# Mamba-2 decay on ScalarE, and one step between VectorE's results and ScalarE's use of them

## The chip, the cores and the metric

The kernel runs on one core of a Trainium2 chip. A core has several engines, each with its own instruction queue that is worked off in order: TensorE (PE, matrix products; PEld are its weight loads), VectorE (DVE), ScalarE (ACT), GpSimd (POOL), and SyncE (SP), which here issues the loads of weights. Instructions of different engines wait for one another through semaphores. The metric is the device time of one execution in microseconds; the time of a kernel is the median over its runs.

## What is computed

The reference is a two-layer trunk over 256 tokens of width 2048: a Mamba-2 layer with a gated feed-forward block, then a block-sparse attention layer with another such block. The change concerns the Mamba-2 mixer alone, and in it the part that works on 64 heads in chunks of 128 tokens:

```
zxbcdt = x @ w_in                       # z, then x, b, c, then dt
xbc = silu(causal_dwconv(xbc, conv_w, conv_b))
dt = softplus(dt + dt_bias); a = -exp(a_log)
...
a_cum = cumsum(a * dt, axis=2)          # per chunk of 128 tokens
seg = a_cum[:, :, :, None] - a_cum[:, :, None, :]
decay_in = exp(where(causal, seg, -inf))
cb = einsum('bclgn,bcsgn->bclsg', c, b)
y_diag = einsum('bclsgr,bcsgrp->bclgrp', cb[..., None] * decay_in, x)
...
y = (y_diag + y_off) + d_skip * xs
y = y * silu(z)
yg = yg * rsqrt(mean(square(yg)) + eps) # over the 512 channels of a head group
y = (yg * norm_w) @ w_out
```

The 64 heads form 8 head groups of 8 heads (512 channels). Since a_cum falls along a chunk, seg is not positive where the mask lets it through.

## The kernel before

**Steps.** The whole kernel is one list of steps. A step takes one tile of weights, 128 x 1024 numbers (512 KB), loaded by SyncE into the buffer `raw` (L170). Because the products are done in a reduced float format, each tile is cut in two: ScalarE copies it to its high part `hi` (L184), VectorE subtracts this from the tile and leaves the low part `lo` (L185). The activations are cut in the same way. In the steps of the Mamba input projection (the function `whole`) TensorE multiplies the high part with both parts of the activations (L244, 8 products of 128x512) and the low part with the high activations (L246, 8 products of 128x256). Steps of even number within a chunk do L244 first, steps of odd number L246 first. Around three eighths of step i, `splits` issues the cutting of a later tile; 4 buffers of each part let the cutting run at most three steps ahead of the product. In the output projection and later (`half`) the three kinds of product stand on L207, L208 and L212.

**Order.** Nothing is scheduled by a planner: the author writes the order by hand. `at(i, f, ...)` appends a function to the list that is run behind the products of step i, and the functions of one step are issued in the order in which they were appended. Each engine then works through its own instructions in that order. So a piece that is put "at step i" stands, on VectorE and ScalarE, behind the cutting issued in step i and ahead of that issued in step i + 1; whoever waits there holds up all later cutting.

**A head group.** Group g has 16 steps from s0 on: 8 for its x columns (chunk `chX[g]`), 8 for its z columns (`chZ[g]`). A chunk's columns come in two halves, ready after 4 and after 8 steps. Some of a group's work reaches into the 16 steps of the next group, or, for the last group, into the output projection `chO`. The pieces that the change touches or that the prediction needs:

- `m_load` (s0+3): GpSimd issues two transfers that spread a_cum of the 8 heads over all partitions into two tiles `mA` of 128 x 8 x 128, one for each chunk of tokens, c = 0 and 1 (L670). They wait until the diagonal products of the group before have read these buffers.
- `m_cb` (s0+6): the products of b and c (L676, L677); VectorE masks them with a triangle into `cb` (L679); ScalarE copies the third into `bc` (L683).
- `m_into` (s0+6): exponentials of a_cum itself for the state that enters chunk 1 (L696), read from `mA` before it is changed; a load of the activation table stands ahead of them.
- `m_decay` (s0+6 for c = 0, s0+7 for c = 1): a subtraction with a broadcast column for each head (L688) and a minimum with 0 (L689), both on VectorE over the whole tile; then `m_exp` one step later each (L700), and `m_mask` (L704), which multiplies the tile by `cb`, at s0+13 and s0+14.
- the convolution over x: `gather` takes a half of the columns out of the accumulators (L554 on ScalarE, L555 on VectorE), a step later `taps` does the first tap on ScalarE (L577) and three on VectorE (L582). `x_silu` follows at s0+11 (L711, with a table load ahead).
- `x_turn` (s0+13): 8 transposes (L720), then xdt and xe on VectorE (L722, L723); `y_d`, 4 pieces on ScalarE (L729).
- `z_silu`: the gather of a half of z and its silu (L757), at s0+12 and s0+16.
- `y_off`, `y_diag` (s0+18): products L746, L737 and the sums L749, L750, L740 on VectorE.
- `z_gate` (s0+20): y times silu(z) on VectorE (L761), its square on ScalarE (L762); `z_sum` (s0+21) adds the squares (L766, L767); `z_rms` (s0+22) takes their mean over the partitions by a product (L773) and GpSimd does the power; `z_diag` (s0+23, L782).
- `z_scale` for group g is put at step s0+13 of group g + 1 (s0+26 for the last group): one product (L787), four pieces on VectorE (L790), then the high and low parts of the result, the copy on ScalarE (L793) and the subtraction on VectorE (L794), which waits for the copy.

Of the kernel before, what the change touches and what calls it, by code (L numbers as in the profile page):

```python
# [20 lines left out]
AF = mybir.ActivationFunctionType  # L21
OP = mybir.AluOpType
AX = mybir.AxisListType

P = 128
# [5 lines left out]
NG = 8  # L31
# [60 lines left out]
def yoco_kernel(ctx: ExitStack, tc: tile.TileContext, x, lmg, lmb, lfg, lfb, x_t, columns, w, out):  # L92
    nc = tc.nc
# [7 lines left out]
    def t4k(name):  # L101
        return t4.tile([P, 2, NC], F32, tag="t4k", name=name)
# [4 lines left out]
    def tp_tile():  # L107
        return psum.tile([P, NC], F32, tag="tp", name="tp", bufs=2)
# [11 lines left out]
    def c1(name, j):  # L120
        i = COL_AT[name] + j
        return cols[:, i:i + 1]
# [174 lines left out]
    def at(i, f, *a):  # L297
        post.setdefault(i, []).append((f, a))
# [172 lines left out]
    chX, chZ = [], []  # L471
# [76 lines left out]
    aux = mp.tile([P, 5, NH], F32, name="aux")  # L548

    def gather(ch, half, dst, scale=None):  # L550

        p = ch.part[half]
        if scale is None:
            nc.scalar.copy(dst, p[:, :, S:])  # L554
            nc.vector.tensor_add(dst, dst, p[:, :, :S])  # L555
        else:
            nc.scalar.activation(dst, p[:, :, S:], AF.Copy, scale=scale)
            nc.vector.scalar_tensor_tensor(dst, p[:, :, :S], scale, dst, op0=OP.mult, op1=OP.add)
# [36 lines left out]
    def conv4(ch, j, dst, jd):  # L595

        return Conv(ch, j, dst, jd, [k * 48 for k in range(4)], "cw", "cb")
# [58 lines left out]
    G = [dict() for _ in range(NG)]  # L656
# [27 lines left out]
        G[g]["cb"], G[g]["bc"] = cb, bc  # L684

    def m_decay(g, c):
        t = G[g]["A", c]
        nc.vector.tensor_sub(t, t, aux[:, 2 + c, 8 * g:8 * g + 8].unsqueeze(2).to_broadcast([P, 8, P]))  # L688
        nc.vector.tensor_scalar(t, t, 0.0, None, op0=OP.min)  # L689

    def m_into(g):

# [4 lines left out]

    def m_exp(g, c):
        t = G[g]["A", c]
        nc.scalar.activation(t, t, AF.Exp)  # L700

    def m_mask(g, c):
        t = G[g]["A", c]
# [2 lines left out]
    def x_new(g):  # L706
        G[g]["xc"] = mp.tile([P, 4, S], F32, tag="xc", name="xc")
        return G[g]["xc"]
# [40 lines left out]
        nc.vector.tensor_mul(e, e, ps.rearrange("p (j l) -> p j l", l=P))  # L749
        nc.vector.tensor_add(y, y, e)  # L750

    def z_silu(g, half):
        if half == 0:
            G[g]["sz"] = t4k("sz").rearrange("p a (k t) -> p (a k) t", t=S)
        sz = G[g]["sz"][:, 2 * half:2 * half + 2, :]
        gather(chZ[g], half, sz)
        nc.scalar.activation(sz, sz, AF.Silu)  # L757

    def z_gate(g):
        y, sz = G[g]["y"], G[g]["sz"]  # L760
        nc.vector.tensor_mul(y, y, sz)  # L761
        nc.scalar.activation(sz, y, AF.Square)  # L762

    def z_sum(g):
        sz = G[g]["sz"]
# [18 lines left out]
    def z_scale(g):  # L784

        ps = tp_tile()
        nc.tensor.matmul(ps[:, :S], ones, G[g]["rd"].rearrange("p h t -> p (h t)"), start=True, stop=True)  # L787
        y = G[g]["y"]
        for i in range(4):
            nc.vector.scalar_tensor_tensor(y[:, i, :], y[:, i, :], c1("nw", 4 * g + i), ps[:, :S], op0=OP.mult,  # L790
                                           op1=OP.mult)
        hi, lo = (yT[:, 4 * g:4 * g + 4, a, :] for a in range(2))
        nc.scalar.copy(hi, y)  # L793
        nc.vector.tensor_sub(lo, y, hi.bitcast(F32))  # L794
# [8 lines left out]
    for g in range(NG):  # L803
        s0 = chX[g].first
        at(s0 + 3, m_load, g)
        at(s0 + 6, m_cb, g)
        at(s0 + 6, m_into, g)
        at(s0 + 6, m_decay, g, 0)
        at(s0 + 7, m_decay, g, 1)
        at(s0 + 7, m_exp, g, 0)  # L810
        at(s0 + 8, m_exp, g, 1)
        conv4(chX[g], 4 * g, lambda g=g: x_new(g), 0).plan()
        at(s0 + 11, x_silu, g)
        at(s0 + 13, m_mask, g, 0)
        at(s0 + 14, m_mask, g, 1)
        if g:
            at(s0 + 13, z_scale, g - 1)
        at(s0 + 13, x_turn, g)
        at(s0 + 13, y_d, g)
        for b in range(2):  # L820
            at(chZ[g].ready(b), z_silu, g, b)
        at(s0 + 18, y_off, g)
        at(s0 + 18, y_diag, g)
        at(s0 + 20, z_gate, g)
        at(s0 + 21, z_sum, g)
        at(s0 + 22, z_rms, g)
        at(s0 + 23, z_diag, g)
    at(s0 + 26, z_scale, NG - 1)


    def chain(norm, nxt=None, after=None):
# [299 lines left out]
```

## Time and profile before

| | us |
|---|---|
| median of 3 runs | 2583.18 |
| lowest, highest | 2579.88, 2583.73 |
| the profiled execution, its run time | 2580.0 |
| the profiled execution, span from its first to its last instruction | 2578.1 |

The profile is of one execution. The Mamba input projection's head groups take the stretch from about 90 to 525 us of it, with work of the last group until about 566 us. Over 54 us of one group in the middle (226 to 280 us) TensorE is busy 51.17 us, VectorE 42.38, ScalarE 31.34 and GpSimd 2.52; the 16 DMA engines are busy 0.55 of the time. In the next projections of the same form (745 to 1200 us) TensorE is busy all of the 455 us. Times in the views are microseconds from the start of the span, unless they are marked or known as nanoseconds (minimum, median and maximum of one instruction are in nanoseconds). In the view that lists instructions in order of time each row has the start, the length, the engine, the line and operation, what it writes and reads with shapes, and how many like instructions were merged; a bracket gives the idle time of that engine just before, and what ended it. A product's end is modelled and overlaps the next one, so busy times of TensorE are somewhat long and its idle times somewhat short.

### The profile page before, as it was taken

How to read it: one execution, taken by the hardware profiler on the slowest of the kernel's cores; microseconds unless marked ns; L12 is line 12 of the kernel's file. 1: busy time of each engine (PE TensorE's matmuls, PEld its weight loads, DVE VectorE, ACT ScalarE, POOL GpSimd, SP SyncE). 2: the span in 40 equal slices, each digit the busy share in tenths (PEclk: the TensorE clock that was granted, in tenths of full speed). 3: DMA queues.
4: the chain of work that ended last, by engine and by line, in shares of the span. 5: the costliest groups of instructions: out<-in, count | busy, mean ns of one | idle time of the engine just before them, and what ended most of it. 6: DMA issues, size and time to landing. Idle time of an engine off the chain costs nothing.

```text
span 2578.1 us, 36030 instructions
## 1 busy us (share of the span) xinstructions
PE 2545.9 (99%) x14031; PEld 2207.3 (86%) x14031; DVE 1680.7 (65%) x2154; ACT 1313.4 (51%) x1633; POOL 71.6 (3%) x89
## 2 busy tenths in 40 slices
PE   9999999999999999999999999999999999999998
PEld 8888888888888888888888888888888888888887
DVE  7877777774576676666444745655777676665555
ACT  6665555543355555555333444544455555554333
POOL 0000000000010000000000200000200000000001
PEclk9999999999999999999999999999999999999999
DMA  7555555557666556565676665456665555566665
GB/s 261 190 183 168 187 181 164 171 188 228 213 206 194 187 189 189 187 193 184 204 227 198 224 191 180 153 166 217 233 196 188 188 188 190 187 195 198 203 221 163
DMA packets 141498, 501.01 MB, mean 194 GB/s; under 512 B 15616, under 2 KB 16128, under 8 KB 141328
## 3 DMA queue, kind: packets, MB, share of 16 engines
q1 hardware_dynamic: 136976, 483.45, 58.2%
q0 software_dynamic: 4064, 14.75, 1.8%
q8 instruction: 110, 1.80, 0.3%
q14 instruction: 60, 0.49, 0.1%
q10 hardware_dynamic: 288, 0.52, 0.1%
HBM read 490.20 MB, written 8.45 MB: 193 GB/s over the span
## 4 chain that ended last, share of the span: by engine, by line
PE 88%; DVE 6%; ACT 3%; issue 2%; DMA 0%; DVEq 0%; SPq 0%; ACTq 0%
PE acc L244 35%; PE acc L246 18%; PE acc L208 11%; PE acc L212 11%; PE acc L207 11%; DVE lo L185 2%; ACT hi L184 2%; PE acc L737 1%; DVE xc L582 1%; DVE y L790 0%; PE tp L212 0%; PE tp L208 0%; PE tp L207 0%; DVE y L761 0%; DVE yT L794 0%
## 5 line engine op out<-in xcount | busy, mean ns | idle before, releaser
L185 DVE TENSOR_TENSOR lo<-raw,hi 128x1024 fp32r<-128x1024 f32 (+1 forms) x871 | 1063.8, 1226 | 763.2 <-ACT hi L184 759.3
L184 ACT CAST hi<-raw 128x1024 fp32r<-128x1024 f32 (+1 forms) x871 | 908.8, 1048 | 863.8 <-PE acc L212 365.8
L244 PE MATMUL acc<-hT,hi 128*128 128x512 f32 x4496 | 1084.3, 392 | 0.4 <-ACT hi L184 0.4
L244 PEld LDWEIGHTS acc<-hT,hi 128*128 128x128 f32 x4496 | 827.5, 189 | 160.8 <-ACT hi L184 1.0
L246 PEld LDWEIGHTS acc<-hT,lo 128*128 128x128 f32 x4496 | 580.7, 191 | 43.1 <-DVE lo L185 18.6
L246 PE MATMUL acc<-hT,lo 128*128 128x256 f32 x4496 | 595.5, 284 | 15.9 <-DVE lo L185 15.9
L208 PE MATMUL acc<-lo,gT 128*128 128x512 f32 (+1 forms) x678 | 254.5, 378 | 0.0
L207 PE MATMUL acc<-hi,gT 128*128 128x512 f32 (+1 forms) x678 | 254.1, 377 | 0.0
L212 PE MATMUL acc<-hi,gT 128*128 128x512 f32 (+1 forms) x678 | 200.6, 377 | 0.0
L207 PEld LDWEIGHTS acc<-hi,gT 128*128 128x128 f32 x678 | 127.6, 188 | 23.3
L208 PEld LDWEIGHTS acc<-lo,gT 128*128 128x128 f32 x678 | 127.6, 188 | 23.2
L212 PEld LDWEIGHTS acc<-hi,gT 128*128 128x128 f32 x678 | 124.9, 188 | 23.6
L208 PE MATMUL acc<-lo,yT 128*128 128x512 f32 (+1 forms) x270 | 98.7, 370 | 1.1 <-DVE lo L185 1.1
L207 PE MATMUL acc<-hi,yT 128*128 128x512 f32 (+1 forms) x270 | 98.9, 371 | 0.6 <-ACT hi L184 0.6
L555 DVE TENSOR_TENSOR u<-u,acc 128x512 f32<-128x512 f32 x108 | 73.5, 681 | 16.4 <-ACT u L554 16.4
L207 PE MATMUL acc<-hi,hT 128*128 128x512 f32 x192 | 78.8, 410 | 0.0
L212 PE MATMUL acc<-hi,yT 128*128 128x512 f32 (+1 forms) x270 | 77.6, 369 | 0.0
L582 DVE SCALAR_TENSOR_TENSOR g<-u,cols,g 128x254 f32<-128x254 f32 (+1 forms) x176 | 73.5, 479 | 5.6 <-ACT g L577 5.6
L208 PE MATMUL acc<-lo,hT 128*128 128x512 f32 x192 | 75.5, 393 | 0.0
L582 DVE SCALAR_TENSOR_TENSOR v<-u,cols,v 128x254 f32<-128x254 f32 (+1 forms) x176 | 73.1, 478 | 0.0
L946 ACT CAST gT<-v 128x512 fp32r<-128x512 f32 x44 | 27.3, 620 | 84.5 <-DVE v L945 84.5
L554 ACT COPY u<-acc 128x512 f32<-128x512 f32 x108 | 62.1, 576 | 0.0
(207 smaller groups left out, 1809.9 us busy)
## 6 DMA issues: line engine op xcount, KB each, us to landing
raw<-in_w SPq DMA_DIRECT2D x881, 512.0 KB, 4.1
mA<-acum_d POOLq DMA_DIRECT2D x16, 512.0 KB, 7.0
hres<-r POOLq DMA_DIRECT2D x12, 512.0 KB, 6.2
r<-hres SPq DMA_DIRECT2D x12, 512.0 KB, 5.1
r<-in_x SPq DMA_DIRECT2D x4, 512.0 KB, 5.1
gb<-in_ln_mix_g SPq DMA_DIRECT2D x8, 256.0 KB, 5.2
gb<-in_ln_mix_b SPq DMA_DIRECT2D x8, 256.0 KB, 5.9
gb<-in_ln_ffn_g SPq DMA_DIRECT2D x8, 256.0 KB, 5.6
```

The costliest lines, as they stand in the source:

```text
L184: nc.scalar.copy(h[:, sl], t[:, sl])
L185: nc.vector.tensor_sub(l[:, sl], t[:, sl], h[:, sl].bitcast(F32))
L207: nc.tensor.matmul(a, th, h[:, kk, sl], start=k == 0, stop=False)
L208: nc.tensor.matmul(a, th, l[:, kk, sl], start=False, stop=False)
L212: nc.tensor.matmul(a, ch.x.lo(k)[:, ts], h[:, kk, sl], start=False, stop=k == ch.nk - 1)
L244: nc.tensor.matmul(banks[j], h[:, kk, js], ch.x.both(k), start=begins, stop=ends, skip_group_check=True)
L246: nc.tensor.matmul(banks[j][:, :S], l[:, kk, js], ch.x.hi(k), start=begins, stop=ends, skip_group_check=True)
L554: nc.scalar.copy(dst, p[:, :, S:])
L555: nc.vector.tensor_add(dst, dst, p[:, :, :S])
L582: nc.vector.scalar_tensor_tensor(d, u[:, i % 2, :S - k], c1(self.at_w, w[n - 1 - k] + self.ia + i), d, op0=OP.mult, op1=OP.add)
L737: nc.tensor.matmul(ps[64 * q:64 * q + 64, c, j * P:(j + 1) * P], G[g]["xdt"][:, c, h * 64:(h + 1) * 64], G[g]["A", c][:, h, :], start=True ...
L946: nc.scalar.copy(h, v[:, sl])
```

## The change

- The decay differences: the subtraction and the minimum on VectorE go. ScalarE does, for each of the 8 heads of a tile, relu(-a_cum + column) on 128 x 128 with that head's column as the bias, and the exponential takes scale -1. Since min(u, 0) = -relu(-u), the result is the same.
- `m_cb` and `m_into` stand at s0+7 instead of s0+6, the exponentials at s0+8 and s0+9 instead of s0+7 and s0+8, the masks at s0+11 and s0+12 instead of s0+13 and s0+14.
- `z_silu` is cut in two: `z_gather` at the old step, the silu one step later. The square moves from `z_gate` into `z_square`, one step later, and `z_sum`, `z_rms` and `z_diag` each stand one step later as well.
- `z_scale` is cut in two: the scaling stays at its step, and the high and low parts (`z_split`) come one step later.

```diff
     def m_decay(g, c):
+
         t = G[g]["A", c]
-        nc.vector.tensor_sub(t, t, aux[:, 2 + c, 8 * g:8 * g + 8].unsqueeze(2).to_broadcast([P, 8, P]))
-        nc.vector.tensor_scalar(t, t, 0.0, None, op0=OP.min)
+        for h in range(8):
+            nc.scalar.activation(t[:, h, :], t[:, h, :], AF.Relu, scale=-1.0, bias=aux[:, 2 + c, 8 * g + h:8 * g + h + 1])
...
     def m_exp(g, c):
         t = G[g]["A", c]
-        nc.scalar.activation(t, t, AF.Exp)
+        nc.scalar.activation(t, t, AF.Exp, scale=-1.0)
...
-    def z_silu(g, half):
+    def z_gather(g, half):
         if half == 0:
             G[g]["sz"] = t4k("sz").rearrange("p a (k t) -> p (a k) t", t=S)
+        gather(chZ[g], half, G[g]["sz"][:, 2 * half:2 * half + 2, :])
+
+    def z_silu(g, half):
         sz = G[g]["sz"][:, 2 * half:2 * half + 2, :]
-        gather(chZ[g], half, sz)
         nc.scalar.activation(sz, sz, AF.Silu)
 
     def z_gate(g):
-        y, sz = G[g]["y"], G[g]["sz"]
-        nc.vector.tensor_mul(y, y, sz)
-        nc.scalar.activation(sz, y, AF.Square)
+        nc.vector.tensor_mul(G[g]["y"], G[g]["y"], G[g]["sz"])
+
+    def z_square(g):
+        nc.scalar.activation(G[g]["sz"], G[g]["y"], AF.Square)
...
         for i in range(4):
             nc.vector.scalar_tensor_tensor(y[:, i, :], y[:, i, :], c1("nw", 4 * g + i), ps[:, :S], op0=OP.mult,
                                            op1=OP.mult)
+
+    def z_split(g):
+        y = G[g]["y"]
         hi, lo = (yT[:, 4 * g:4 * g + 4, a, :] for a in range(2))
         nc.scalar.copy(hi, y)
         nc.vector.tensor_sub(lo, y, hi.bitcast(F32))
...
     for g in range(NG):
         s0 = chX[g].first
         at(s0 + 3, m_load, g)
-        at(s0 + 6, m_cb, g)
-        at(s0 + 6, m_into, g)
+        at(s0 + 7, m_cb, g)
+        at(s0 + 7, m_into, g)
         at(s0 + 6, m_decay, g, 0)
         at(s0 + 7, m_decay, g, 1)
-        at(s0 + 7, m_exp, g, 0)
-        at(s0 + 8, m_exp, g, 1)
+        at(s0 + 8, m_exp, g, 0)
+        at(s0 + 9, m_exp, g, 1)
         conv4(chX[g], 4 * g, lambda g=g: x_new(g), 0).plan()
         at(s0 + 11, x_silu, g)
-        at(s0 + 13, m_mask, g, 0)
-        at(s0 + 14, m_mask, g, 1)
+        at(s0 + 11, m_mask, g, 0)
+        at(s0 + 12, m_mask, g, 1)
         if g:
             at(s0 + 13, z_scale, g - 1)
+            at(s0 + 14, z_split, g - 1)
         at(s0 + 13, x_turn, g)
         at(s0 + 13, y_d, g)
         for b in range(2):
-            at(chZ[g].ready(b), z_silu, g, b)
+            at(chZ[g].ready(b), z_gather, g, b)
+            at(chZ[g].ready(b) + 1, z_silu, g, b)
         at(s0 + 18, y_off, g)
         at(s0 + 18, y_diag, g)
         at(s0 + 20, z_gate, g)
-        at(s0 + 21, z_sum, g)
-        at(s0 + 22, z_rms, g)
-        at(s0 + 23, z_diag, g)
+        at(s0 + 21, z_square, g)
+        at(s0 + 22, z_sum, g)
+        at(s0 + 23, z_rms, g)
+        at(s0 + 24, z_diag, g)
     at(s0 + 26, z_scale, NG - 1)
+    at(s0 + 27, z_split, NG - 1)
```

## The prediction

> **What bounds the kernel now.** I read the page first, for the share of each engine.
>
> ```profile
> span 2578.1 us, 36030 instructions
> PE 2545.9 (99%) x14031; PEld 2207.3 (86%) x14031; DVE 1680.7 (65%) x2154; ACT 1313.4 (51%) x1633; POOL 71.6 (3%) x89
> ```
>
> TensorE is busy for all but 32 us, so only TensorE's idle time and its clock can be gained or lost. Next I asked who TensorE waits for (line, releaser, total us, times, longest), in the Mamba stretch from 85 to 580 us:
>
> ```profile
> PE acc L246 <- DVE lo L185: 15.9, 13, 2.2
> ...
> PE acc L208 <- DVE lo L185: 1.1, 1, 1.1
> PE acc L207 <- ACT hi L184: 0.6, 1, 0.6
> ```
>
> All 13 waits of L246 in the whole run lie in that stretch: TensorE stands because VectorE is late with a low half of a weight tile. The chain of waits shows how often. A piece of 16 matmuls of L244 covers the high products of two neighbouring steps, so two such pieces 5.56 us apart give 2.78 us a step; the later six rows are the same place in successive head groups.
>
> ```profile
> 94.37 3.65 PE acc L244 x16
> 99.93 3.65 PE acc L244 x16
> ...
> 226.53 3.67 PE acc L244 x16
> 280.23 3.67 PE acc L244 x16
> ...
> 335.49 3.67 PE acc L244 x16
> ...
> 390.69 3.67 PE acc L244 x16
> ...
> 444.38 3.67 PE acc L244 x16
> ...
> 499.65 3.67 PE acc L244 x16
> ```
>
> A group takes 53.70 us, and three times 55.26, 55.20 and 55.27. In one of those three the windows view has this row (TensorE's granted clock third from the right):
>
> ```profile
> 311.00:318.00 7.00, 6.55 (x27) 5.55 (x28) 5.37 (x6) 3.66 (x6) 0.00 (x0) 0.76 0.67 204
> ```
>
> The clock falls to 0.76 right behind that group's stall: about 1.55 us lost three times, 4.6 us in all. Inside one group TensorE's timeline shows the places (start, length, and in brackets the idle time before). I number the steps of group g from its first x step, s0. The step at 225.33 is s0+7, 242.82 is s0+13, 257.75 is s0+17 and 266.30 is the step behind the group's y products; 121.67 and 158.92 are the same two ends, s0+7 and s0+19, in group 0.
>
> ```profile
> 121.67 1.20 PE L246 MATMUL acc<-hT,lo 128*128 128x256 f32 x8
> ...
> 158.92 1.21 PE L246 MATMUL acc<-hT,lo 128*128 128x256 f32 x8
> ```
>
> ```profile
> 224.22 0.58 PE L773 MATMUL tp<-mean,sz 128*128 128x1 f32 x4 [0.24 <-DVE sz L767]
> ...
> 225.33 1.20 PE L246 MATMUL acc<-hT,lo 128*128 128x256 f32 x8
> ...
> 242.82 1.22 PE L246 MATMUL acc<-hT,lo 128*128 128x256 f32 x8 [0.38 <-DVE lo L185]
> ...
> 254.43 1.11 PE L246 MATMUL acc<-hT,lo 128*128 128x256 f32 x8
> ...
> 257.75 1.22 PE L246 MATMUL acc<-hT,lo 128*128 128x256 f32 x8 [2.21 <-DVE lo L185]
> ...
> 266.30 1.21 PE L246 MATMUL acc<-hT,lo 128*128 128x256 f32 x8
> ```
>
> Three stalls a group. (a) 0.24 before the mean product. (b) Six steps of 2.78 from 225.33 end at 242.02, and s0+13 starts at 242.82: 0.80 lost. (c) Eight low products take 0.96 from start to start (1.11 with the tail of the last), so s0+16 ends at 255.39, and s0+17 starts at 257.75: 2.36 lost. Group 0 needs 37.25 us from s0+7 to s0+19 where this group needs 40.97: (b), (c) and the one product of z_scale, which group 0 doesn't have, are the difference. So a group from 1 to 6 loses 3.40 us. For group 7, s0+17 lies in the output projection, and its (c) is the 1.1 and 0.6 us of L208 and L207.
>
> **Stall (c): masks and the split.** VectorE's timeline between the low half for s0+16 and that for s0+17:
>
> ```profile
> 249.64 1.22 DVE L704 TENSOR_TENSOR mA<-mA,cb 128x1024 f32<-128x1024 f32 x1
> 250.77 1.65 DVE L790 SCALAR_TENSOR_TENSOR y<-y,cols,tp 128x256 f32<-128x256 f32 x4
> 253.54 1.22 DVE L794 TENSOR_TENSOR yT<-y,yT 128x1024 fp32r<-128x1024 f32 x1 [1.12 <-ACT yT L793]
> 254.68 1.28 DVE L722 TENSOR_TENSOR xdt<-acc,aux 128x512 f32<-128x512 f32 x2
> 255.88 0.68 DVE L723 TENSOR_TENSOR xe<-xdt,aux 128x512 f32<-128x512 f32 x1
> 256.48 1.22 DVE L185 TENSOR_TENSOR lo<-raw,hi 128x1024 fp32r<-128x1024 f32 x1
> ```
>
> 6.84 us pass from the mask to the low half. The change takes the mask (1.13 from start to start) to s0+11, and the wait for ScalarE with the subtraction behind it (253.54 less 250.77 and 1.65, then 1.14: 2.26) behind the low half of s0+17. 3.4 us go, and (c) is 2.36: it vanishes with about 1 us to spare. Where the moved work lands it needs cover. The masks, 2.3 us, fall at s0+11 and s0+12, into VectorE's queue that loses more than this through the decay lines, which come before them:
>
> ```profile
> L688 DVE TENSOR_TENSOR mA<-mA,aux x16: 1217/1218/1221, 122.4 to 506.6; 128x1024 f32<-128x1024 f32 x16
> ```
>
> Two of those (2.4 us) and two minimum passes go. Had the masks no cover they would add at most their own 2.3 us to (b). z_split at s0+14 puts ScalarE's copy, which waits for z_scale, in front of the high half for s0+18; that half has two whole steps (5.6 us) left. The silu after the z gather, and the square after the gate, go one step back: their ScalarE waits no longer hold the high half behind them, and (a) goes too, because the sum is now read a step later. I take nothing more for these: each is the same instruction one step later, and uncovered it would hold up a high half by its own length, as it does now. z_rms and m_cb change steps but not length.
>
> **Stall (b): decay on ScalarE.** Nothing in the old trace is a relu of 128x128 with a bias column. Nearest rows: an exponential of 128 elements with such a bias, and an affine of 256 elements with two columns, followed by ScalarE's timeline of that same group and of group 0:
>
> ```profile
> L644 ACT ACTIVATE tb<-tb x1: 406/406/406, 86.4 to 86.4; 64x128 f32<-64x128 f32 x1
> ```
>
> ```profile
> L577 ACT ACTIVATE xc<-u,cols x32: 587/595/607, 115.9 to 511.5; 128x256 f32<-128x256 f32 x32
> ```
>
> ```profile
> 122.47 0.27 ACT L683 COPY bc<-tp 128x128 f32<-128x128 f32 x1 [2.87 <-DVE cb L679]
> ```
>
> ```profile
> 228.01 0.27 ACT L683 COPY bc<-tp 128x128 f32<-128x128 f32 x1 [4.32 <-DVE cb L679]
> ...
> 230.87 1.05 ACT L184 CAST hi<-raw 128x1024 fp32r<-128x1024 f32 x1
> ...
> 235.52 1.06 ACT L700 ACTIVATE mA<-mA 128x1024 f32<-128x1024 f32 x1 [1.71 <-DVE mA L689]
> ...
> 237.91 1.09 ACT L577 ACTIVATE xc<-u,cols 128x256 f32<-128x256 f32 x2
> ```
>
> Two L577 take 1.09 where one takes 0.595, so neighbours overlap by 0.10. One relu is 0.406, a run of eight 7 x 0.306 + 0.406 = 2.55 us. Bounds: 0.17 apart (L683's 0.27 less the overlap), 1.4 us; 0.50 apart (L577's, twice the elements), 4.1 us. I take 2.55, since L644 has the same 128 elements and the same bias. The first eight run at s0+6 where ScalarE now sits idle 4.32 us before L683: hidden; without that cover they'd cost their 2.55. The second eight stand at s0+7 behind L683 and the exponential of m_into, and the high half for s0+11, both big exponentials and the taps of L577 queue behind them; VectorE's taps L582 wait for L577, and the low half for s0+13, which is stall (b), waits behind L582:
>
> ```profile
> 238.04 1.22 DVE L185 TENSOR_TENSOR lo<-raw,hi 128x1024 fp32r<-128x1024 f32 x1 [0.26 <-ACT hi L184]
> 239.18 2.45 DVE L582 SCALAR_TENSOR_TENSOR xc<-u,cols,xc 128x255 f32<-128x255 f32 x6
> ```
>
> From L683 to L577 is 9.90 us now. The 1.71 wait for VectorE's decay goes, one L184 (0.95 net) moves ahead of L683, eight relus (2.45 net) come in: 9.69. But m_cb is a step later. Now L683 runs 0.10 before s0+8 starts (225.33 + 2.78 = 228.11); afterwards it comes as in group 0, where nothing delays it: 0.80 behind the start of the step that follows the m_cb products (122.47 against 121.67). So L577 starts at s0+8 plus 10.49 instead of plus 9.80, 0.69 later. L582 now starts 1.27 behind L577, because a low half stands before it; with VectorE free earlier it starts when the first L577 is done, 0.62 behind: 0.65 regained. Net 0.04: (b) stays, 0.84 in place of 0.80, and group 0, whose decay ran free, gets it new.
>
> **The sum.** Groups 1 to 6: 0.24 + 2.36 - 0.04 = 2.56 each, 15.4. Group 7: 0.24 + 1.7 - 0.04 = 1.9. Group 0: minus 0.84. Clock: 4.6, as a stall of 0.84 is a third of the one that the dips follow. Together 21.1 us. Behind the Mamba stretch TensorE is the bound, so all of it reaches the end. The span becomes 2578.1 - 21.1 = 2557.0, and with the 1.9 us that the profiled run (2580.0) has beside its span, 2559 us. The median of the runs shown (2583.18) lies 3.2 above the profiled run; by 1.55 each that would be two more clock dips (an estimate), and these should go as well, so I add nothing.
>
> **Rivals.**
> *The clock dips stay.* For it: seven stalls of like length, only three dips, so the stall alone isn't their cause. Against: the dip shown begins right behind its stall. Price 4.6 us: 2563.5. The Trainium skill (TensorE: Matmul & The Clock Gate, What's actually happening) puts the throttled clock behind at least one idle window of about 3.4 us; by that 2.2 us shouldn't trip it, the dips have another cause, and 2563.5 would be the sum. The trace rather speaks for the stall, 0.76 behind 2.2 idle us.
>
> *ScalarE's second eight cost more.* At 0.50 apart they add 1.5 us to (b), 12 us over eight groups: 2571, and 2576 if the clock dips as well. At 0.17 apart they take 1.1 off: (b) nearly gone, 2552.
>
> *Slower: ScalarE becomes the pace of s0+7 to s0+13.* One mechanism: the second run of eight relus between L683 and L577. It decides once it takes 21.1/8 = 2.6 us a group more than 2.55, that is 5.2 us or 0.65 a relu, and the run is back at 2580; at 0.80 a relu, 1.2 us a group more, it is 2590. Against: 0.65 is above 0.595 for twice the elements. The Trainium skill (ScalarE: Activation LUTs, Rules for kernel authors) says to put relu, max and min on VectorE and not on ScalarE; as bare work the rows agree, 2.55 against 1.22 and a minimum pass. It would be right about the time if ScalarE were the late engine.
>
> *The mA transfer is not there.* ScalarE reads mA at s0+6 with no product ahead of it.
>
> ```profile
> 212.12 0.92 POOL L670 DMA_DIRECT2D mA<-acum_d  x1 [37.35 <-DVE lo L185]
> ```
>
> ```profile
> DMA to landing us min/median/max: 5.1/7.0/8.6
> ```
>
> Issued at 212.12, landed by 220.7 at worst; ScalarE gets there when its idle time before L683 begins, 228.01 - 4.32 = 223.7, or some 1.4 us sooner. A late landing would first eat that idle time. It needs 8 us more than the longest seen to cancel the gain.
>
> *The change does not do what it says:* relus that each force a table load. In the instruction order of the changed kernel ScalarE has the same two loads a group, so no.
>
> **Chances.** Forecast, 2552 to 2562: 0.66. Dips stay or dearer relus, 2562 to 2576: 0.22. ScalarE as the pace, over 2583: 0.06. mA late, or a stall at another step that eats the gain: 0.06, half about as before, half slower. The range 2550 to 2573 holds the first and most of the second. 0.2% (5.2 us) is about what can be told from no change: faster 0.88, the same 0.04, slower 0.08.
>
> **What would show it.** Right: s0+8 rows of the chain some 51 us apart in all groups, none 55; no wait over 2 us on L185, the rest under 1 us at s0+13 (or s0+11), also in group 0; the clock 1.00 in the Mamba stretch; relu near 0.40 us; no TensorE wait at the mean product. Wrong: relus over 0.6 us, the idle time of L246 above 10 us in total, ScalarE waiting for the mA transfer, or dips at 0.76 without a long stall ahead.

## The result, and the profile after

The changed kernel takes 2555.32 us (median of 4 runs, 2554.92 to 2556.50) against 2583.27 before (4 runs): a ratio of 0.9895, 95% interval 0.9878 to 0.9913. It is faster by 28 us, or 1%; 2559 was forecast, within 2550 to 2573. One execution of the later run d2_rest_only took 4621.31 us at a granted clock of 0.77; it is left out of that run's median, and as it is the profiled one, the run has no span below.

The page of the changed kernel, its span and the busy times of the engines:

```profile
span 2554.6 us, 36102 instructions
PE 2536.9 (99%) x14031; PEld 2202.6 (86%) x14031; DVE 1653.5 (65%) x2122; ACT 1355.1 (53%) x1761; POOL 71.5 (3%) x89
```

23.5 us of span are gone. VectorE has 27 us less work and ScalarE 42 us more, so in sum the engines work more than before. What TensorE waited for (line, releaser, total us, times, longest):

```profile
PE acc L246 <- DVE lo L185: 3.6, 8, 0.5
```

15.9 us in 13 waits have become 3.6 in 8, one in each group, group 0 included, and the longest is 0.5 us instead of 2.2. The mean product has no wait any more. The chain of waits at the same place in successive groups (the last row is four groups behind the third):

```profile
161.70 3.65 PE acc L244 x16
...
212.38 3.65 PE acc L244 x16
...
263.07 3.65 PE acc L244 x16
...
465.82 3.65 PE acc L244 x16
```

Each group takes 50.69 us, none 55. From 161.70 to 465.82 six periods make 304.1 us, where the same six took 326.8 (172.85 to 499.65): 22.7 of the 23.5 us, as six times 3.01 us of stall and the 4.6 us of the three clock dips. The granted clock (third from the right) bears this out. The first row is a group with a dip before the change, the second a group after it; after it all of them show 1.00:

```profile
280.00:335.00 55.00, 52.16 (x316) 45.52 (x316) 41.90 (x57) 31.46 (x40) 2.52 (x3) 0.97 0.53 172
```

```profile
223.00:274.00 51.00, 50.56 (x321) 44.72 (x320) 38.97 (x54) 36.89 (x58) 2.51 (x3) 1.00 0.58 187
```

Inside a group, TensorE's timeline; 239.29 is the low half of s0+12, 240.85 that of s0+13, and 252.46 joins those of s0+16 and s0+17:

```profile
225.19 0.50 PE L777 MATMUL tp<-mean,sz 128*128 128x1 f32 x4
...
226.22 2.10 PE L244 MATMUL acc<-hT,hi 128*128 128x512 f32 x8
...
239.29 1.11 PE L246 MATMUL acc<-hT,lo 128*128 128x256 f32 x8
240.85 1.22 PE L246 MATMUL acc<-hT,lo 128*128 128x256 f32 x8 [0.44 <-DVE lo L185]
...
252.46 2.08 PE L246 MATMUL acc<-hT,lo 128*128 128x256 f32 x16
```

Stall (c) is gone: the two low halves at s0+16 and s0+17 run as one piece. Stall (b) is 240.85 less 239.29 and 0.96, that is 0.60 us. VectorE's timeline shows why (c) went; the low half for s0+17 is the row at 250.44:

```profile
245.94 1.22 DVE L185 TENSOR_TENSOR lo<-raw,hi 128x1024 fp32r<-128x1024 f32 x1
247.07 1.65 DVE L794 SCALAR_TENSOR_TENSOR y<-y,cols,tp 128x256 f32<-128x256 f32 x4
248.64 1.29 DVE L723 TENSOR_TENSOR xdt<-acc,aux 128x512 f32<-128x512 f32 x2
249.84 0.69 DVE L724 TENSOR_TENSOR xe<-xdt,aux 128x512 f32<-128x512 f32 x1
250.44 1.23 DVE L185 TENSOR_TENSOR lo<-raw,hi 128x1024 fp32r<-128x1024 f32 x1
251.57 1.23 DVE L801 TENSOR_TENSOR yT<-y,yT 128x1024 fp32r<-128x1024 f32 x1
```

Neither a mask nor the wait for the copy stands between the two low halves; 4.50 us lie between their starts, where 6.84 passed from the mask alone to the second of them. The later one ends at 251.67, 1.75 us before TensorE comes to it (252.46 and 0.96). The subtraction of the split comes behind. ScalarE at s0+7 to s0+9, with the eight relus of chunk 1 as one row, and the relu's own row (minimum, median and maximum in ns):

```profile
226.97 0.27 ACT L683 COPY bc<-tp 128x128 f32<-128x128 f32 x1 [2.75 <-DVE cb L679]
...
229.85 2.46 ACT L690 ACTIVATE mA<-mA,aux 128x128 f32<-128x128 f32 x8
...
236.49 1.08 ACT L577 ACTIVATE xc<-u,cols 128x256 f32<-128x256 f32 x2
```

```profile
L690 ACT ACTIVATE mA<-mA,aux x128: 384/388/404, 120.3 to 485.4; 128x128 f32<-128x128 f32 x128
```

A relu is 0.388 us, eight are 2.46, and L577 starts 9.52 us behind L683.

### The profile page after: what moved, and what is told of

It is laid out like the page before. It is cut to its first block, busy times and chain, and to the rows that moved or that the text cites. A ratio compares the mean times of both kernels' runs of the same rounds, so it can differ in the third digit from the quotient of the medians.

```text
span 2554.6 us, 36102 instructions
## 1 busy us (share of the span) xinstructions
PE 2536.9 (99%) x14031; PEld 2202.6 (86%) x14031; DVE 1653.5 (65%) x2122; ACT 1355.1 (53%) x1761; POOL 71.5 (3%) x89
## 4 chain that ended last, share of the span: by engine, by line
PE 93%; ACT 3%; DVE 2%; issue 1%; DMA 0%; SPq 0%; DVEq 0%; ACTq 0%
PE acc L244 37%; PE acc L246 20%; PE acc L208 11%; PE acc L212 11%; PE acc L207 11%; DVE lo L185 1%; ACT hi L184 1%; ACT mA L690 1%; DVE xc L582 1%; PE acc L738 1%; DMA raw<-in_w 0%; PE tp L212 0%; PE tp L208 0%; PE tp L207 0%; ACT L697 0%
## 5 line engine op out<-in xcount | busy, mean ns | idle before, releaser
L185 DVE TENSOR_TENSOR lo<-raw,hi 128x1024 fp32r<-128x1024 f32 (+1 forms) x871 | 1064.6, 1227 | 775.3 <-ACT hi L184 770.4
L246 PE MATMUL acc<-hT,lo 128*128 128x256 f32 x4496 | 589.3, 283 | 3.6 <-DVE lo L185 3.6
L582 DVE SCALAR_TENSOR_TENSOR g<-u,cols,g 128x254 f32<-128x254 f32 (+1 forms) x176 | 73.6, 479 | 6.0 <-ACT g L577 6.0
L555 DVE TENSOR_TENSOR u<-u,acc 128x512 f32<-128x512 f32 x108 | 73.4, 681 | 0.8 <-ACT u L554 0.8
L582 DVE SCALAR_TENSOR_TENSOR v<-u,cols,v 128x254 f32<-128x254 f32 (+1 forms) x176 | 73.2, 479 | 0.0
```

What stands on the lines that cost most here:

```text
L185: nc.vector.tensor_sub(l[:, sl], t[:, sl], h[:, sl].bitcast(F32))
L246: nc.tensor.matmul(banks[j][:, :S], l[:, kk, js], ch.x.hi(k), start=begins, stop=ends, skip_group_check=True)
L582: nc.vector.scalar_tensor_tensor(d, u[:, i % 2, :S - k], c1(self.at_w, w[n - 1 - k] + self.ia + i), d, op0=OP.mult, op1=OP.add)
```

## The experiments

The forecast had added up stalls. Two questions were left: which part of the change brings the gain, and whether the order of the queues (theory A) or VectorE's load (theory B) explains it. Times are medians, and ratios are against the kernel before on the same chip. The lowest time of the kernel before was 2579.45 to 2579.88 us in each of the four sets of runs, so the rows can also be compared with one another. Spans are those of the one profiled execution.

| run | what it is | us | ratio (95% interval) | span |
|---|---|---|---|---|
| d1_relu_only | before, decay on ScalarE | 2598.88 | 1.0068 (1.0053 to 1.0083) | 2597.0 |
| d3_masks_only | before, masks two steps sooner | 2582.08 | 1.0003 (0.9993 to 1.0012) | 2579.8 |
| d4_lag_only | before, the three lags | 2549.61 | 0.9877 (0.9862 to 0.9891) | 2547.4 |
| d2_rest_only | changed, decay back on VectorE | 2549.56 | 0.9876 (0.9859 to 0.9892) | |
| d11_rest_again | the same, for its trace | 2549.27 | 0.9868 (0.9826 to 0.9911) | 2547.5 |
| d5_split_only | before, only the split later | 2559.88 | 0.9917 (0.9902 to 0.9932) | 2558.1 |
| d9_silu_only | before, only the silu later | 2564.09 | 0.9934 (0.9919 to 0.9949) | 2562.9 |
| d10_square_only | before, only the square and what follows later | 2558.49 | 0.9912 (0.9897 to 0.9927) | 2556.7 |
| d8_exp_later | changed, exponentials another step later | 2549.67 | 0.9877 (0.9861 to 0.9894) | 2548.9 |
| d6_c0_twice | changed, relus of chunk 0 twice | 2578.76 | 0.9988 (0.9977 to 1.0000) | 2575.7 |
| d7_c1_twice | changed, relus of chunk 1 twice | 2588.03 | 1.0021 (1.0009 to 1.0032) | 2586.6 |

### The decay on ScalarE alone (d1_relu_only)

```diff
     def m_decay(g, c):
-        nc.vector.tensor_sub(t, t, aux[:, 2 + c, 8 * g:8 * g + 8].unsqueeze(2).to_broadcast([P, 8, P]))
-        nc.vector.tensor_scalar(t, t, 0.0, None, op0=OP.min)
+        for h in range(8):
+            nc.scalar.activation(t[:, h, :], t[:, h, :], AF.Relu, scale=-1.0, bias=aux[:, 2 + c, 8 * g + h:8 * g + h + 1])
...
-        nc.scalar.activation(t, t, AF.Exp)
+        nc.scalar.activation(t, t, AF.Exp, scale=-1.0)
```

> The kernel before with the decay on ScalarE (relu with bias, exponential with scale -1) and nothing else. Theory A (order): stalls (b) and (c) hang on one chain from L683 over L577 and L582 on to the low half of s0+17; here all sixteen relus (4.9 us) stand in it, the 1.7 us wait for VectorE goes and 0.65 us comes back on VectorE: +2.5 us a group, also in group 0, so a span of about 2597 (2590 to 2603), slower than before. Theory B (load): VectorE was too full, and 3.8 us less of work on it for each group takes the stalls away: about 2556.

It is slower by 18 us, and the span is the 2597 of theory A. TensorE's timeline of one group of this run (the first row is s0+11, the second s0+17):

```profile
244.48 1.22 PE L246 MATMUL acc<-hT,lo 128*128 128x256 f32 x8 [2.44 <-DVE lo L185]
...
265.28 1.21 PE L246 MATMUL acc<-hT,lo 128*128 128x256 f32 x8 [2.21 <-DVE lo L185]
```

The stall at s0+17 is the same 2.21 us as before, though VectorE has nearly 4 us less to do in each group, and a second one of 2.44 us stands at s0+11. VectorE's load wasn't the cause; theory B falls.

### The masks alone (d3_masks_only)

```diff
-        at(s0 + 13, m_mask, g, 0)
-        at(s0 + 14, m_mask, g, 1)
+        at(s0 + 11, m_mask, g, 0)
+        at(s0 + 12, m_mask, g, 1)
```

> The kernel before with the masks at s0+11 and s0+12 and nothing else. Theory A: the first mask leaves the stretch between the low halves of s0+16 and s0+17 (1.13 us), but the second now stands ahead of the gather of z, whose silu on ScalarE holds up the high half for s0+16, 1.13 us later: no change, 2578 within 4. Theory B: 1.1 us a group less of stall (c): about 2569.

No change. VectorE's timeline of this run, from the second mask on; the row at 251.53 is the low half for s0+16, 258.38 begins with that for s0+17:

```profile
248.08 1.22 DVE L704 TENSOR_TENSOR mA<-mA,cb 128x1024 f32<-128x1024 f32 x1
249.22 0.68 DVE L555 TENSOR_TENSOR sz<-sz,acc 128x512 f32<-128x512 f32 x1
251.53 1.23 DVE L185 TENSOR_TENSOR lo<-raw,hi 128x1024 fp32r<-128x1024 f32 x1 [1.63 <-ACT hi L184]
...
258.38 3.49 DVE L185 TENSOR_TENSOR lo<-raw,hi 128x1024 fp32r<-128x1024 f32 x3
```

The second mask stands ahead of L555, the silu waits for L555, the next high half stands behind the silu, and VectorE idles 1.63 us for that half: what the masks free on one side of it they cost on the other.

### The lags alone (d4_lag_only), and all but the relu (d2_rest_only, d11_rest_again)

d4_lag_only has the new `z_gather`, `z_square` and `z_split` and their steps; `m_decay` and `m_exp` are those before the change. Against the changed kernel its other steps are:

```diff
-        at(s0 + 7, m_cb, g)
-        at(s0 + 7, m_into, g)
+        at(s0 + 6, m_cb, g)
+        at(s0 + 6, m_into, g)
...
-        at(s0 + 8, m_exp, g, 0)
-        at(s0 + 9, m_exp, g, 1)
+        at(s0 + 7, m_exp, g, 0)
+        at(s0 + 8, m_exp, g, 1)
...
-        at(s0 + 11, m_mask, g, 0)
-        at(s0 + 12, m_mask, g, 1)
+        at(s0 + 13, m_mask, g, 0)
+        at(s0 + 14, m_mask, g, 1)
```

> The kernel before with only the step between VectorE's results and ScalarE's use of them: silu of z, square, sum, mean, diag and the split of z_scale one step later; decay on VectorE, products, exponentials and masks at their old steps. Theory A: the low half of s0+17 comes some 4 us sooner, so (a) and (c) go and the clock dips with them; (b) stays 0.80: span about 2556 (2553 to 2559). Theory B: VectorE has all its old work, so most of the stall stays: 2568 or more.

2547.4: faster than either theory said, and faster than the whole change by 7 us of span (5.7 in the medians). In the Mamba stretch TensorE waits for nothing; its groups in the chain of waits:

```profile
210.19 3.65 PE acc L244 x16
...
260.19 3.65 PE acc L244 x16
```

50.0 us a group, so (b) is gone too, which I had left at 0.80. ScalarE's copy of `bc` in this run shows how:

```profile
222.35 0.27 ACT L683 COPY bc<-tp 128x128 f32<-128x128 f32 x1 [3.62 <-DVE cb L679]
```

s0+8 begins at 224.03 here, behind the mean product, so L683 comes 1.7 us ahead of it, where it was 0.10 ahead before the change. Which lag does this, d10_square_only shows below.

The other side of the cut keeps every step of the change and only puts the two lines of `m_decay` and the plain exponential back:

> The changed kernel with the decay differences back on VectorE (subtraction and minimum) and the exponential without a scale; all steps as changed. Theory A: the eight relus of chunk 1 leave the chain from L683 to L577, L577 comes some 1.7 us sooner, the 0.60 us stall at s0+13 goes in all eight groups: span about 2550 (2548 to 2553), faster than the changed kernel. Theory B: VectorE gets 3.8 us a group back and is late again: 2562 or more.

> The changed kernel with the decay back on VectorE again, for its trace. Theory A: no TensorE wait on L185 in the Mamba stretch, groups 50.0 us apart, L577 about 8 us behind L683 instead of 9.5; span 2548 within 1.

2549.56 and 2549.27: as fast as the lags alone, about 6 us faster than the change. No wait on L185 is left. L577 follows L683 by 7.16 us, not 9.52:

```profile
225.60 0.27 ACT L683 COPY bc<-tp 128x128 f32<-128x128 f32 x1 [4.88 <-DVE cb L679]
...
232.76 1.08 ACT L577 ACTIVATE xc<-u,cols 128x256 f32<-128x256 f32 x2
```

So the relus on ScalarE and the earlier masks add nothing to the gain, and at the steps of the change the relus cost what stall (b) costs. L683 comes 1.4 us behind s0+8 in d11 (224.22), later than in the changed kernel: without the relus that is early enough.

### One lag at a time (d5_split_only, d9_silu_only, d10_square_only)

The split is cut off from `z_scale` in d5, the silu from the gather of z in d9, the square from `z_gate` in d10:

```diff
+    def z_split(g):
+        y = G[g]["y"]
...
             at(s0 + 13, z_scale, g - 1)
+            at(s0 + 14, z_split, g - 1)
...
+    at(s0 + 27, z_split, NG - 1)
```

```diff
             at(chZ[g].ready(b), z_silu, g, b)
+            at(chZ[g].ready(b) + 1, z_silu1, g, b)
```

```diff
-        at(s0 + 21, z_sum, g)
-        at(s0 + 22, z_rms, g)
-        at(s0 + 23, z_diag, g)
+        at(s0 + 21, z_square, g)
+        at(s0 + 22, z_sum, g)
+        at(s0 + 23, z_rms, g)
+        at(s0 + 24, z_diag, g)
```

> The kernel before with only the split of z_scale one step later (s0+14, and s0+27 for the last group). Theory A: 2.26 us leave VectorE's stretch between the low halves of s0+16 and s0+17, so (c) shrinks from 2.36 to about 0.1 us in groups 1 to 7, the clock dips go with it, (a) and (b) stay: span about 2558 (2555 to 2563). Rival: the three later steps only work together, because (c) is the end of one long chain, and each alone gives little: 2570 or more.

> The kernel before with only the silu of z one step behind its gather. Theory A: ScalarE no longer waits for VectorE's sum ahead of the high half for s0+16; that comes 1.7 us sooner, (c) shrinks to about 0.7 us and no longer trips the clock: span about 2562 (2558 to 2568). Rival as for the split alone: 2570 or more.

> The kernel before with only the square, the sum, the mean and the diagonal one step later. Theory A: the product for cb no longer queues behind the mean product, L679 no longer behind taps, a low half and L775, so L683 and L577 come about 1.1 us sooner; (a) goes, (b) goes (0.80), and (c) becomes about 2.0 us: 1.5 us each in seven groups, span about 2568, and about 2564 if a stall of 2.0 us no longer trips the clock. Rival: this lag only moves (a), 0.24 us a group: 2576.

The spans are 2558.1, 2562.9 and 2556.7. The first two are what theory A said. For the split the low products of s0+16 and s0+17 nearly close up:

```profile
252.37 2.19 PE L246 MATMUL acc<-hT,lo 128*128 128x256 f32 x16
```

(2.19 where 2.08 is undisturbed). The silu alone leaves 0.78 us of (c), counted as the 2.36 was (254.88 less 253.14 and 0.96); theory A said 0.7. The third gave 11 us more than expected, 7 more than for the case that the dips go: no stall at s0+13, and at s0+17 1.20 us (253.38 less 251.22 and 0.96) instead of 2.0.

```profile
251.22 1.11 PE L246 MATMUL acc<-hT,lo 128*128 128x256 f32 x8
253.38 1.22 PE L246 MATMUL acc<-hT,lo 128*128 128x256 f32 x8 [1.05 <-DVE lo L185]
```

VectorE's timeline of this run has the reason, with the sum (L768, L769) now behind the taps (L582) and the product for `cb` (L679) right after it:

```profile
220.91 0.47 DVE L582 SCALAR_TENSOR_TENSOR xc<-u,cols,xc 128x253 f32<-128x253 f32 x1
221.30 1.22 DVE L185 TENSOR_TENSOR lo<-raw,hi 128x1024 fp32r<-128x1024 f32 x1
222.44 0.68 DVE L768 TENSOR_TENSOR sz<-sz 128x512 f32<-128x512 f32 x1
223.15 0.43 DVE L769 TENSOR_TENSOR sz<-sz 128x256 f32<-128x256 f32 x1
223.50 0.42 DVE L679 TENSOR_TENSOR cb<-tp,tri 128x256 f32<-128x256 f32 x1
```

```profile
223.95 0.27 ACT L683 COPY bc<-tp 128x128 f32<-128x128 f32 x1 [3.56 <-DVE cb L679]
```

In the kernel before, the square (L762) stands on ScalarE ahead of the gather of x, waits for VectorE's gate (L761), and VectorE's part of the gather (L555) waits in its turn:

```profile
219.28 1.06 ACT L762 ACTIVATE sz<-y 128x1024 f32<-128x1024 f32 x1 [2.49 <-DVE y L761]
```

```profile
220.84 0.69 DVE L555 TENSOR_TENSOR u<-u,acc 128x512 f32<-128x512 f32 x1 [1.66 <-ACT u L554]
```

So it holds up gather, taps, a low half and L679 in a row. One step later it stands behind the gather, and L683 comes 1.7 us ahead of s0+8 (225.68) instead of 0.10. Alone the three lags bring 20, 15 and 21 us of span; together they bring 31, as any one of them already ends the clock dips (each group of all four runs shows a granted clock of 1.00), and as they shorten the same stalls, which can't be cut below zero.

### The exponentials a step later (d8_exp_later)

```diff
-        at(s0 + 8, m_exp, g, 0)
-        at(s0 + 9, m_exp, g, 1)
+        at(s0 + 9, m_exp, g, 0)
+        at(s0 + 10, m_exp, g, 1)
```

> The changed kernel with the two exponentials another step later (s0+9 and s0+10). Theory A: one exponential (0.96 us) leaves the stretch of ScalarE between L683 and L577, so L577 and the low half of s0+13 come 0.96 us sooner and the stall of 0.60 us at s0+13 goes in all eight groups: span about 2550 (2549 to 2551). Rival: ScalarE is simply full from s0+7 to s0+13, and the stall moves on to the silu and the high half for s0+15: 2553 to 2555.

2549.67 us, no wait in the Mamba stretch, with all relus on ScalarE. It beats the changed kernel and equals the lags alone. In the group that I read ScalarE works in this run from L683 at 226.25 until 246.67 without a gap of 0.1 us, and still no half of a weight tile is late. So stall (b) wasn't ScalarE's load as such: one exponential less in the queue between L683 and L577 ends it.

### The relus twice (d6_c0_twice, d7_c1_twice)

In d7 the condition is c == 1.

```diff
+        if c == 0:
+            dummy = mp.tile([P, P], F32, tag="dummy", name="dummy", bufs=1)
+            for h in range(8):
+                nc.scalar.activation(dummy, t[:, h, :], AF.Relu, scale=-1.0, bias=aux[:, 2 + c, 8 * g + h:8 * g + h + 1])
```

> The changed kernel with the eight relus of chunk 0 done twice (the first time into a scratch tile that nothing reads): 2.4 us more of ScalarE at s0+6 in each group. Theory A: they fall into the 2.75 us in which ScalarE waits ahead of L683: span 2554.6 within 1. Theory C (ScalarE's load as such sets the time from s0+6 to s0+13): plus 2.4 us in eight groups, 2574.

> The changed kernel with the eight relus of chunk 1 done twice (the first time into a scratch tile that nothing reads): the same 2.4 us, but behind L683 and the exponential of m_into. Theory A: they stand in the chain from L683 over L577 to the low half of s0+13 with no slack, part of the stall shows already at s0+11: plus 2.4 us in eight groups, 2574 (2571 to 2576, more only if the clock dips). If that chain isn't the bound (theory B, VectorE's load): 2554.6 within 2.

Both missed. In part the probe is dearer than planned: its relus run 0.42 us apart, not 0.29, and add 3.34 us, not 2.4. All eight write one tile, which is the likely reason, but no run shows it apart. For chunk 1 this then fits: the stall moves to s0+11, whose low half had only 0.18 us to spare in the changed kernel, and is 3.16 us (300.60 less 296.48 and 0.96),

```profile
296.48 1.11 PE L246 MATMUL acc<-hT,lo 128*128 128x256 f32 x8
300.60 1.24 PE L246 MATMUL acc<-hT,lo 128*128 128x256 f32 x8 [3.01 <-DVE lo L185]
301.66 5.42 PE L244 MATMUL acc<-hT,hi 128*128 128x512 f32 x16
```

2.56 more than 0.60, in eight groups 20.5 us; the remaining 11.5 of the 32.0 us of span fit the clock dips of seven groups, as in the last row (16 products in 5.42 us, otherwise 3.82). For chunk 0 theory A is refuted as I had put it: the 2.75 us that ScalarE idles ahead of L683 don't hide the work. The rows of ScalarE and VectorE in this run (L692 are the added relus):

```profile
225.80 3.44 ACT L692 ACTIVATE dummy<-mA,aux 128x128 f32<-128x128 f32 x8
...
231.48 1.03 ACT L184 CAST hi<-raw 128x1024 fp32r<-128x1024 f32 x1
...
234.21 0.27 ACT L683 COPY bc<-tp 128x128 f32<-128x128 f32 x1 [1.69 <-DVE cb L679]
```

```profile
232.55 1.22 DVE L185 TENSOR_TENSOR lo<-raw,hi 128x1024 fp32r<-128x1024 f32 x1 [3.40 <-ACT hi L184]
233.69 0.15 DVE L783 TENSOR_SCALAR rr<-tp 128x2 f32<-128x2 f32 x1
233.76 0.41 DVE L679 TENSOR_TENSOR cb<-tp,tri 128x256 f32<-128x256 f32 x1
```

L683 waits for L679, which on VectorE stands behind a low half, and that waits for the high half which ScalarE's added relus have just put off. ScalarE waits, by way of VectorE, for itself. The real slack is what VectorE idles behind that low half in the changed kernel itself, whose timeline has it in brackets:

```profile
225.73 0.16 DVE L779 TENSOR_SCALAR rr<-tp 128x2 f32<-128x2 f32 x1 [0.25 <-PE tp L777]
226.51 0.42 DVE L679 TENSOR_TENSOR cb<-tp,tri 128x256 f32<-128x256 f32 x1 [0.62 <-PE tp L677]
```

0.87 us by these two. By the starts it is 1.07: L683 comes 3.02 us behind s0+8 in d6 (234.21 less 231.19, its start there), 0.75 in the changed kernel, so 2.27 of the 3.34 us go through. The stall moves to s0+11 here too, 2.15 us in this group (241.80 less 238.69 and 0.96) instead of 0.60 at s0+13, in eight groups 12.4 us; the remaining 8.7 of the 21.1 us of span fit the clock dips of five groups.

## Why the prediction was right, point by point

- *Stall (c), right.* It was to vanish with 1 us to spare, and it vanished. The runs show more: the split alone takes off nearly all of it, and the masks take off nothing on their own. The prediction's 3.4 us was one sum of both, and 2.26 of it, the split, is what a run confirms; d4 loses (c) with the masks at their old steps. The silu's lag, taken at nothing, by itself cuts (c) from 2.36 to 0.78 (d9), and so the changed kernel has 1.75 us to spare.
- *The cover for the masks, unnecessary.* The prediction said the decay lines make room on VectorE. With those lines back (d2, d11) the masks still fit.
- *Stall (b), right in mechanism, 0.84 forecast and 0.69 measured.* That is the period of 50.69 less the 50.00 of d4, which has no stall; 0.60 of it stands at s0+13 itself. The relus are 0.388 instead of 0.406 us, the path from L683 to L577 9.52 instead of 9.69, and L683 comes 0.75 (226.97 less 226.22) instead of 0.80 behind the start of s0+8. Group 0 got the stall that it hadn't had. That it takes the second eight relus is shown by d11, and that it takes the exponential beside them by d8; in both it is gone. What the later step of m_cb and m_into adds to it was not run alone.
- *The first eight relus, right, with less to spare than it said.* They cost nothing, but the reason, 4.32 us of ScalarE idle time, was wrong as a measure: with them in place 1.07 us of slack are left (d6), where ScalarE shows 2.75 us idle. The 8 us that the rival of the late transfer was given rest on the same idle time.
- *The lags taken at nothing, wrong in part.* The prediction gave the square's lag only the 0.24 us of (a). In the kernel before it also brings the gather, the taps and L683 forward by some 1.6 us a group and ends (b) (d10). The sum escaped this: for the changed kernel it took L683's place from group 0, where no square stands ahead of it, and that place was nearly right (0.80 forecast, 0.75 measured). What it missed is that without the later m_cb and the relus the lag would have taken (b) away.
- *Stall (a), right, larger than its row.* In the old trace the low products of s0+6 start at 222.87 and take 0.96, and the mean product starts at 224.22: 0.39 us, not the 0.24 that the wait shows.
- *The clock, right.* No dip is left. The old profile has three groups of 55 us, the new one none. The old trace has six stalls of 2.2 us, not the seven like stalls that the prediction counts; the seventh is the 1.1 and 0.6 us of the output projection. The medians differ by 27.95 us where the spans differ by 23.5: 1.2 of the 4.45 us between is the profiled execution after, the slowest of its four, and 3.3 is the median before against its profiled execution. The latter fits the two further dips that the prediction read into the median: of 34 other executions of the kernel before, the 13 with a mean granted clock of 0.997 took 2579.45 to 2580.55 us, the 9 with 0.995 2582.44 to 2583.89.
- *The sum:* 21.1 forecast, 23.5 measured. Against the 50.00 us of d4, each of groups 1 to 6 lost 3.7 us before (beside the dips) and 0.7 after, 3.01 less; the forecast had 3.40 and 0.84, 2.56 less. In six groups that is 2.7 us too little; the rest of the kernel gave 0.3 less than forecast.
- *The rivals.* The Trainium skill's rule to put relu on VectorE and not on ScalarE (ScalarE: Activation LUTs, Rules for kernel authors) didn't decide the whole, but for its part it was right here: d1 shows 18 us lost by the move alone, and d11 6 us gained by undoing it. But d8 shows that the move cost nothing once the exponentials stood a step later. ScalarE as the pace from s0+7 to s0+13 was the right danger: with 3.34 us more there, d7 is slower than the kernel before. The mA transfer was not waited for.

## What to carry to other kernels

In queues written out by hand, look first for an instruction that waits for another engine with unrelated work of the critical path behind it, and put one step between producer and consumer; three such shifts, with no work moved, gave more than the whole change. Idle time of an engine is slack only if what ends it doesn't depend on that engine's own earlier work. Moving work to a less busy engine is no gain as such: test each part of a bundle alone.

## What the runs showed of the hardware

In the Mamba stretch the TensorE clock fell only behind longer stalls, and there not each time. With waits of 0.4 to 0.6 us (changed kernel, d5, d9) and of 1.05 us (d10) the granted clock was 1.00 in each group. Behind 2.0 us (d6, groups 1 to 7) it fell in 4 of 7 groups, behind 2.4 (d6, group 0) in 1 of 1, behind 2.2 in 3 of 6 (before) and in 4 of 6 (d3), behind 3.0 (d7) in 7 of 8. Why it falls in one group and not in the next, these runs don't show. Two groups of d6 with waits of 1.99 and 2.02 us, the granted clock third from the right:

```profile
292.00:312.00 20.00, 18.01 (x100) 15.58 (x99) 17.27 (x26) 18.38 (x27) 0.00 (x0) 0.91 0.48 159
346.00:366.00 20.00, 17.52 (x103) 15.22 (x102) 17.41 (x26) 18.45 (x28) 0.00 (x0) 1.00 0.51 157
```

A dip costs about 1.55 us. By the Trainium skill (TensorE: Matmul & The Clock Gate, What's actually happening) the clock is throttled after at least one idle window of about 3.4 us. These runs don't agree: they show it behind 2.0 us of waiting. The dips go with a scatter of the times: 14 runs of the kernel before lie between 2579.58 and 2584.51, the 4 of d4, which has no dip, between 2549.37 and 2549.72.
